# Mixer front of a hybrid encoder trunk: all weight differences on VectorE, long convolution on 24 stretches of 16 tokens

## The chip, the cores and the metric

The kernel runs on one core of one Trainium2 chip. The metric is the device time of one execution in microseconds (us); the time before is the median of three runs. The engines are named as in the profile: PE is TensorE (matmuls), DVE is VectorE, ACT is ScalarE, POOL is GpSimd, SP is SyncE, which issues almost all DMAs.

## The reference

Two layers of a streaming encoder run on 384 tokens: one prompt of 256 tokens and 8 sample streams of 16 tokens. All of it is float32. Cut to what matters:

```
x += 0.5 * rmsnorm(SwiGLU(rmsnorm(x)))          first FFN, D = 1024, D_FF = 2816
n  = rmsnorm(x);  h = n @ w_in                  columns for attention, conv, gMLP, short conv, 4 gates
  a  = latent attention; prompt: softmax over 256 keys in chunks, samples: 256 cached + 16 keys
  xb = ga * sigmoid(gg)                         two 256-channel parts of h
  yb = silu(layernorm(causal_dwconv(concat(buf_b, xb), conv_b_w) + bias))    31 taps per channel
  yc = u * spatial_mix(layernorm(v));  yd = bg * causal_dwconv(cg * hd)      3 taps
  y  = sum_b sigmoid(gate_b) * (branch_b @ w_br_b);  x += rmsnorm(y @ w_o)
x += 0.5 * rmsnorm(SwiGLU(rmsnorm(x)))          second FFN
```

The long convolution (31 taps) reads 30 tokens of history: zeros before the prompt, `state_conv_b` before each sample stream. Its last 30 inputs per stream are outputs too.

## The kernel before

The 384 tokens are three tiles of 128. PE multiplies in a split form: every float32 operand is a rounded high part and the low rest, and three products are added (high x high, low x high, high x low), so each weight is turned into two tiles. A weight unit (mostly 128 x 1024) is loaded by SP into a stage buffer `st` (four buffers, `STAGE`), ACT rounds it into `wh`, and a subtraction `wl = st - wh` gives the rest (`split_unit`, L237). Both lie in a ring in SBUF (`RING_M` KB per partition during the mixer), and PE's products wait for them.

The program is written in the order of a planner's time. `tick` (L184) counts PE's work; what waits for another engine is a generator that goes on when the planner thinks that engine is through. `pump` (L268) prepares the next weight unit when its ring place is free and when ACT and the subtracting engine are at most `BACKLOG` = 400 ns behind, or when fewer than `AHEAD` = 3 units are ready. Each engine then works through its own queue strictly in this order. One list, `self.idle`, holds the taps of the long convolution: `tick` puts one into DVE's queue whenever the planner sees DVE free within 100 ns.

The mixer's front (`mixer_front`) is, in the order of PE: token-major projections (`cq`, then `ckv` and `v`), the first half of the convolution's projections (`conv(0)`), eight query heads (`query`, L934), `conv(1)`, prompt keys and values (`kT`, `v`), then six chains of prompt attention (scores, softmax, transposes, product with `v`) and eight of sample attention, with the remaining feature-major projections (`fillers`) between them. After that comes the merge of the four branches.

From the queries on (`self.pool_split`, L946 to L1167) the subtractions `wl` of the front are POOL's, 20 units per layer; elsewhere they are DVE's. POOL also adds the rotated parts of the queries: two small additions per head, `qTp` and `qr`.

A tap of the long convolution (`taps`, L675) is two instructions for each of two channel chunks: 256 prompt tokens from the buffer `bp` (30 zeros of history, then 256 tokens in a row) and 8 x 16 sample tokens from `bs` (each stream with its own 30 tokens of history). There are 31 taps and two chunks, so 62 taps and 124 instructions per layer; each is `y = x * w + y` with x and y in SBUF, apart from the first tap.

In the rows, `yTb` is the convolution's result, `half` a scratch tile (softmax probabilities among others), `rot` and `acc` PSUM tiles. All instructions of the engines carry line L72, since they are issued through one helper.

Of the kernel before, what the change touches and what calls it, by code (L numbers as in the profile page):

```python
# [16 lines left out]
P = 128  # L17
# [9 lines left out]
S = 16  # L27
PAST = 256
# [10 lines left out]
RING_M = 39  # L39
# [5 lines left out]
POOL_SPLIT = True  # L45
# [14 lines left out]
class Engine:  # L60
    """an engine whose work is counted as it is emitted"""
# [36 lines left out]
class Core:  # L98
# [5 lines left out]
    def plan_units(self):  # L104
        """every weight unit in the order of its use: (key, DRAM AP, shape without partitions)"""
        units = []
        a = self.a
        for l in range(self.depth):
            for f in ("ffn1", "ffn2"):
                if f == "ffn2":  # L110
                    self.plan_mixer(units, l)
                for h in range(4):
                    units.append(((f, l, "s", h), a[f + "_gs"][l, :, 2 * h:2 * h + 2, :], [2, 512],
                                  "F" if f == "ffn2" or l == 0 else "M"))
                order = []
                for c in range(2, NC_FF):
                    order.append(("p", c))
                    if c >= LAG:
                        order.append(("d", c - LAG))
                order += [("d", c) for c in range(NC_FF - LAG, NC_FF)]  # L120
                for k, c in order:
                    if k == "p":
                        for h in range(2):
                            units.append(((f, l, "p", c, h), a[f + "_gp"][l, c - 2, h], [KD, P], "F"))
                    else:
                        units.append(((f, l, "d", c), a[f + "_dn"][l, c * P:(c + 1) * P, :], [D], "F"))
        return units

    # The program is emitted in the order of time. `now` is the tensor engine's work emitted so far, free[e] the time
    # at which another engine is through with its own. What waits for another engine is a generator: it yields the  # L130
    # engine it waits for (or a time) and goes on when that is through, so that others' work comes in between.
# [6 lines left out]
    def spawn(self, name, gen, kind=None):  # L138
        """start a generator; it holds what its parent holds, and the tiles of that kind taken since the last such start"""
        parent = self.cur  # L140
        if parent is None or parent[:len(name)] != name:
            self.seq += 1
            name = name + (self.seq,)
            for slot, names in self.holders.items():
                if parent in names or (parent is None and slot in self.fresh.get(kind, ())):
                    names.add(name)
            self.old.add(kind)
        else:
            name = parent
        busy, self.busy = self.busy, True  # L150
        self.step(name, gen)
        self.busy = busy

    def take(self, slot):
        """before a tile goes into a slot: emit all that still uses the one there"""
        while names := [n for n in self.holders.get(slot, ()) if n != self.cur and self.pending(n)]:
            self.need(names[0])
        self.holders[slot] = {self.cur} - {None}
        if self.cur is None:
            if slot[0] in self.old:  # L160
                self.old.discard(slot[0])
                self.fresh[slot[0]] = set()
            self.fresh.setdefault(slot[0], set()).add(slot)

    def drop(self, kind):
        """the running generator is through with its tiles of that kind"""
# [31 lines left out]
    def need(self, name):  # L198
        """emit until all generators of that name are through"""
# [10 lines left out]
    def wait(self, name, gen):  # L210
        """need(name), with gen's work in between"""
# [25 lines left out]
    def split_unit(self, key, shape, ring, st, n, arrival):  # L237
# [3 lines left out]
        e = POOL if self.pool_split else DVE  # L241
# [4 lines left out]
        getattr(nc, e).tensor_tensor(lo, st, h.bitcast(F32), op=ALU.subtract)  # L246
# [11 lines left out]
    def places(self, ring, n):  # L258
        """where the next two tiles of n bytes lie in the ring, and where it goes on"""
# [8 lines left out]
    def pump(self):  # L268
        """the next unit, if its place in the ring is free by now"""
        if self.next_unit < len(self.units):  # L270
# [5 lines left out]
            lag = max(self.free[ACT], self.free[POOL if self.pool_split else DVE]) - self.now  # L276
# [28 lines left out]
    def mm3(self, out, lhs, rhs, first, last):  # L305
        """out += (lh + ll)^T (rh + rl), without ll rl"""
# [5 lines left out]
    def stat(self, tag, n):  # L312
        """n columns of per-row statistics"""
# [34 lines left out]
    def load_gain(self, ap):  # L348
        """a gain of every column, the same in all partitions"""
# [4 lines left out]
    # The tiles' chains across a boundary: the last products of a sublayer run tile by tile, so a tile's norms  # L354
    # run beside the other tiles' products, and so do the first products of the next sublayer.
    def tails(self, tail, post, gain):
        """tail[t]: the last products of tile t, of its two halves; post: its post-norm; then the pre-norm with gain"""
# [31 lines left out]
    def chain(self, t, post, stats, gain, at=None):  # L389
        """the rest of the post-norm, then xT[:, :, tile t] <- the transpose of the normalised residual"""  # L390
# [65 lines left out]
    def ffn_head(self, f, l):  # L456
        """the first two pairs of gate and up chunks, token-major"""
# [32 lines left out]
    def ffn_body(self, f, l, out=None, hook=None):  # L490
        """the other chunks; returns what the boundary needs: the products left, tile by tile, and the post-norm"""
# [112 lines left out]
    def softmax(self, p, s, n):  # L604
        """p[:, i, :] = softmax of s[:, i, :] over the last axis"""
# [12 lines left out]
    def mixer(self, l, m):  # L618
        """returns what the boundary after it needs"""
# [17 lines left out]
    def mixer_front(self, l, m, mf, ma, aT, yT):  # L637
# [15 lines left out]
        # feature-major projections and the three local branches  # L653
# [12 lines left out]
        bp = mf.tile([P, 2, BW + TP], F32, name="bp")  # L666
        bs_ = mf.tile([P, 2, NB, BW + S], F32, name="bs")
        dp = mf.tile([P, 2, DW + TP], F32, name="dp")
        ds_ = mf.tile([P, 2, NB, DW + S], F32, name="ds")
        nc.gpsimd.memset(bp[:, :, 0:BW], 0.0)  # L670
        nc.gpsimd.memset(dp[:, :, 0:DW], 0.0)
        nc.sync.dma_start(out=bs_[:, :, :, 0:BW], in_=a["stateb"][l])
        nc.sync.dma_start(out=ds_[:, :, :, 0:DW], in_=a["stated"][l])

        def taps(y, pad_p, pad_s, w, ks, bias):  # L675
            for k in ks:
                for e, dst, src in ((nc.vector, y[:, :TP], pad_p[:, k:k + TP]), (nc.vector, samp(y), pad_s[:, :, k:k + S])):
                    wk = w[:, k:k + 1]
                    if k:
                        e.scalar_tensor_tensor(dst, src, wk, dst, op0=ALU.mult, op1=ALU.add)  # L680
                    elif bias is not None:
                        e.tensor_scalar(dst, src, wk, bias, op0=ALU.mult, op1=ALU.add)
                    else:
                        e.tensor_scalar(dst, src, wk, None, op0=ALU.mult)

        y = yT["b"]

# [14 lines left out]
        def conv_glu(c, xa, sg):  # L702
            yield PE
            nc.vector.tensor_tensor(bp[:, c, BW:], xa[:, :TP], sg[:, :TP], op=ALU.mult)
            nc.vector.tensor_tensor(bs_[:, c, :, BW:], samp(xa), samp(sg), op=ALU.mult)
            nc.sync.dma_start(out=a["o_cbp"][l, :, c], in_=bp[:, c, TP:])
            nc.sync.dma_start(out=a["o_cbs"][l, :, c], in_=bs_[:, c, :, S:])
            for k in range(CW):
                self.idle.append(lambda k=k: taps(y[:, c, :], bp[:, c, :], bs_[:, c], cw[:, c, :], [k], cbias[:, c:c + 1]))
# [15 lines left out]
        def short_conv(c, t_, xh_):  # L725
# [3 lines left out]
            taps(yT["d"][:, c, :], dp[:, c, :], ds_[:, c], dw[:, c, :], range(3), None)  # L729
# [36 lines left out]
        def conv_norm():  # L766
            """layer norm over the channels (two partition chunks), then silu"""
# [57 lines left out]
        with pool("mixq") as mq:  # L825
# [6 lines left out]
            # token-major projections: cq | kr, then ckv | v  # L832
# [11 lines left out]
            def latent_q(t):  # L844
# [3 lines left out]
                # the latents' norm, the rotated key part  # L848
# [29 lines left out]
            def latent_kv(t, pb):  # L878
                tt = slice(t * P, (t + 1) * P)
                yield PE  # L880
                # normalised kv latents
# [21 lines left out]
            def gmlp_v(t, pb):  # L903
                """gMLP's normalised v"""
# [26 lines left out]
            # queries: per head 64 nope, 32 rope, the 32 rope columns with their halves swapped  # L931
# [14 lines left out]
            self.pool_split = POOL_SPLIT  # L946
# [15 lines left out]
            # prompt keys and values  # L962
# [30 lines left out]
            # prompt attention  # L993
# [37 lines left out]
            # what the sample attention reads first  # L1031
# [30 lines left out]
        # sample attention, in the latent space; the rope part of four batches runs in four row groups  # L1062
# [104 lines left out]
        self.pool_split = False  # L1167
# [3 lines left out]
    def gate(self, l, c, g, th):  # L1171
        """th = tanh(gate / 2)"""
# [14 lines left out]
    def mixer_merge(self, l, q, aT, yT, mh, ml):  # L1187
        """gates are 2 sigmoid = tanh(g / 2) + 1; the factor 2 goes out in the post-norm"""
# [62 lines left out]
    def rms_stats(self, x, tag):  # L1251
        """the sum of x^2 over its columns, and room for what follows"""
# [4 lines left out]
    def run(self):  # L1257
# [6 lines left out]
        self.pool_split = False  # L1264
# [5 lines left out]
        with ExitStack() as es:  # L1270
# [29 lines left out]
            one = const.tile([P, P], F32, name="one")  # L1300
# [45 lines left out]
class Post:  # L1346
    """x += rmsnorm(h) * gain / 2 for acc = h (FFN); x += rmsnorm(h) * gain for acc = 2 h (mixer)"""
# [35 lines left out]
def lay_out(inp, np):  # L1383
    """the kernel's DRAM arrays: the inputs, re-laid"""
# [51 lines left out]
    # the queries' table carries the scale of the scores  # L1436
# [10 lines left out]
def lay_back(o, np):  # L1447
    """the reference's outputs from the kernel's DRAM arrays"""
# [27 lines left out]
```

## Time and profile before

| | before |
|---|---|
| median of 3 runs | 1942.73 us (1938.77 to 1946.91) |
| span of the profiled execution | 1946.8 us; the run nearest to it is 1946.91 us |
| PE busy | 1883.2 us, 97% |
| DVE busy | 986.1 us, 51% |
| ACT busy | 690.0 us, 35% |
| POOL busy | 155.2 us, 8%, nearly all of it in the two mixer fronts |
| granted TensorE clock, mean | 0.981 |

PE is busy almost throughout; the time that it is not lies in two stretches, the mixer fronts of layer 0 (about 280 to 500 us) and layer 1 (about 1240 to 1465 us). A granted clock of 1 is 2.4 GHz, and 0.5 is 1.2 GHz; a value between them is a mean over a stretch with both.

### The profile page before, as it was taken

The page shows a single profiled execution, that of the slowest core. Times are in us where ns is not written, and L with a number is a line of the kernel's source. Part 1 is how long each engine was busy: PE and PEld are TensorE (multiplying, and loading weights), DVE is VectorE, ACT ScalarE, POOL GpSimd, SP SyncE. Part 2 cuts the span into 40 slices and gives each one's busy share as a digit, 9 for nine tenths or more (in the row PEclk, how much of TensorE's full clock was granted, in tenths as well). Part 3 has the DMA queues.
Part 4 walks back from the last instruction along what each step waited for, and adds up shares of the span by engine and source line. Part 5 has one row for each costly group of instructions (what it writes and reads, how often), then busy time and mean ns, then how long its engine had stood idle before and what let it go on. Part 6 is the DMA issues. An engine that isn't in the chain of part 4 may idle for free.

```text
span 1946.8 us, 25315 instructions
## 1 busy us (share of the span) xinstructions
PE 1883.2 (97%) x10066; PEld 1745.3 (90%) x10066; DVE 986.1 (51%) x1560; ACT 690.0 (35%) x1138; POOL 155.2 (8%) x156
## 2 busy tenths in 40 slices
PE   8999999789999999999999999997899999999998
PEld 7999998677999989999989999986789998899997
DVE  5333357984544473333463333579735444633333
ACT  5333343332433353333343333433223334433322
POOL 0000002522100000000000000025220000000000
PEclk9999999888999999999999999998889999999999
DMA  7434444442343354434444434443423344433341
GB/s 255 131 120 129 127 125 112 117 122 86 106 133 124 115 173 128 129 121 130 130 133 128 130 121 129 127 118 84 138 69 114 114 138 144 141 127 123 130 124 50
DMA packets 99000, 243.13 MB, mean 125 GB/s; under 512 B 29249, under 2 KB 40641, under 8 KB 98882
## 3 DMA queue, kind: packets, MB, share of 16 engines
q1 hardware_dynamic: 98738, 241.45, 40.4%
q8 instruction: 79, 1.29, 0.3%
q14 instruction: 39, 0.32, 0.1%
q10 hardware_dynamic: 144, 0.07, 0.0%
HBM read 237.62 MB, written 3.31 MB: 124 GB/s over the span
## 4 chain that ended last, share of the span: by engine, by line
PE 90%; DVE 9%; issue 1%; ACT 1%; POOL 0%; DMA 0%; POOLq 0%; DVEq 0%; ACTq 0%
PE rot L72 57%; PE acc L72 33%; DVE yTb L72 4%; DVE half L72 1%; DVE yTd L72 1%; DVE qTp L72 0%; DVE sx L72 0%; ACT qTs L72 0%; DVE vn L72 0%; DVE qr L72 0%; DVE xl L72 0%; DVE wl L72 0%; ACT junk L72 0%; DVE kT L72 0%; DVE sv L72 0%
## 5 line engine op out<-in xcount | busy, mean ns | idle before, releaser
L72 DVE TENSOR_TENSOR wl<-st,wh 128x1024 fp32r<-128x1024 f32 (+2 forms) x388 | 456.6, 1185 | 470.2 <-ACT wh L72 449.1
L72 PE MATMUL rot<-xh,wh 128*128 128x384 f32 x1984 | 678.4, 342 | 0.1
L72 PE MATMUL rot<-xh,wl 128*128 128x384 f32 x1984 | 675.6, 341 | 0.0
L72 PE MATMUL rot<-xl,wh 128*128 128x384 f32 x1984 | 674.7, 340 | 0.0
L72 ACT CAST wh<-st 128x1024 fp32r<-128x1024 f32 (+3 forms) x428 | 430.3, 1016 | 668.4 <-issue 374.1
L72 PEld LDWEIGHTS rot<-xh,wh 128*128 128x128 f32 x1984 | 375.7, 189 | 7.4 <-issue 2.9
L72 PEld LDWEIGHTS rot<-xh,wl 128*128 128x128 f32 x1984 | 375.4, 189 | 5.0 <-issue 0.7
L72 PEld LDWEIGHTS rot<-xl,wh 128*128 128x128 f32 x1984 | 375.3, 189 | 2.9 <-issue 1.9
L72 PE MATMUL acc<-wh,hl 128*128 128x512 f32 x528 | 205.8, 390 | 0.0
L72 PE MATMUL acc<-wl,hh 128*128 128x512 f32 x528 | 205.7, 390 | 0.0
L72 PE MATMUL acc<-wh,hh 128*128 128x512 f32 x528 | 205.5, 389 | 0.0
L72 POOL TENSOR_TENSOR post<-post,neghalf 128x1 f32<-128x1 f32 x18 | 12.0, 668 | 1420.2 <-DVE post L72 1420.2
L72 DVE TENSOR_TENSOR hf<-sg,rot 128x384 f32<-128x384 f32 x80 | 44.3, 554 | 152.9 <-PE rot L72 152.9
L72 PEld LDWEIGHTS acc<-wl,hh 128*128 128x128 f32 x528 | 99.1, 188 | 20.5
L72 PEld LDWEIGHTS acc<-wh,hl 128*128 128x128 f32 x528 | 99.1, 188 | 17.6
L72 PEld LDWEIGHTS acc<-wh,hh 128*128 128x128 f32 x528 | 99.1, 188 | 17.6
L72 POOL TENSOR_TENSOR wl<-st,wh 128x1024 fp32r<-128x1024 f32 (+2 forms) x40 | 92.1, 2309 | 182.3 <-ACT wh L72 82.1
L72 DVE SCALAR_TENSOR_TENSOR half<-half,acc 128x384 f32<-128x384 f32 x44 | 24.4, 554 | 140.4 <-PE acc L72 140.4
L72 ACT ACTIVATE half<-rot 128x384 f32<-128x384 f32 x58 | 28.5, 492 | 177.0 <-PE rot L72 177.0
L72 DVE SCALAR_TENSOR_TENSOR yTb<-bp,cols,yTb 128x256 f32<-128x256 f32 x120 | 78.6, 655 | 0.3
L72 PE MATMUL acc<-ident,half 128*128 128x128 f32 (+1 forms) x266 | 44.2, 285 | 20.8 <-DVE half L72 20.8
L72 PEld LDWEIGHTS acc<-ident,half 128*128 128x128 f32 (+1 forms) x266 | 32.9, 142 | 31.8 <-DVE half L72 21.4
(214 smaller groups left out, 1835.5 us busy)
## 6 DMA issues: line engine op xcount, KB each, us to landing
st<-ffn_gp SPq DMA_DIRECT2D x160, 512.0 KB, 3.5
st<-ffn_dn SPq DMA_DIRECT2D x88, 512.0 KB, 3.5
st<-in_g SPq DMA_DIRECT2D x64, 512.0 KB, 4.0
st<-in_f SPq DMA_DIRECT2D x24, 512.0 KB, 3.7
st<-ffn_gs SPq DMA_DIRECT2D x16, 512.0 KB, 4.9
st<-w_o SPq DMA_DIRECT2D x16, 512.0 KB, 4.7
st<-w_br SPq DMA_DIRECT2D x16, 384.0 KB, 3.1
st<-in_b SPq DMA_DIRECT2D x8, 512.0 KB, 4.7
```

Of the source, the lines that this page charges most:

```text
L72: r = f(*args, **kw)
```

## The change

All subtractions `wl` go to DVE, and the planner's lag is that of ACT and DVE. The buffer `bp` is gone: the prompt is held as 16 stretches of 16 tokens, each with its own 30 tokens of history, in front of the 8 sample streams in one buffer `bs` of 24 stretches x 46. DVE writes the 24 x 16 new values in one instruction; ACT then copies each stretch's history out of the stretches before it, in two copies. A tap is one instruction over 24 x 16 = 384 values. The ring for the mixer's weights shrinks from 39 to 36 KB per partition to make room, and a constant tile `one` borrows a scratch tile. Comments are taken out, which changes nothing.

```diff
-RING_M = 39
+RING_M = 36
-POOL_SPLIT = True
@@ split_unit
-        e = POOL if self.pool_split else DVE
...
-        getattr(nc, e).tensor_tensor(lo, st, h.bitcast(F32), op=ALU.subtract)
+        nc.vector.tensor_tensor(lo, st, h.bitcast(F32), op=ALU.subtract)
@@ pump
-            lag = max(self.free[ACT], self.free[POOL if self.pool_split else DVE]) - self.now
+            lag = max(self.free[ACT], self.free[DVE]) - self.now
@@ mixer_front
-        bp = mf.tile([P, 2, BW + TP], F32, name="bp")
-        bs_ = mf.tile([P, 2, NB, BW + S], F32, name="bs")
+        bs_ = mf.tile([P, 2, NP + NB, BW + S], F32, name="bs")
...
-        nc.gpsimd.memset(bp[:, :, 0:BW], 0.0)
+        nc.gpsimd.memset(bs_[:, :, 0, 0:BW], 0.0)
+        nc.gpsimd.memset(bs_[:, :, 1, 0:BW - S], 0.0)
-        nc.sync.dma_start(out=bs_[:, :, :, 0:BW], in_=a["stateb"][l])
+        for c in range(2):
+            nc.sync.dma_start(out=bs_[:, c, NP:, 0:BW], in_=a["stateb"][l, :, c])
...
+        by16 = lambda x: x.rearrange("p (b s) -> p b s", s=S)
+        def tap(c, k):
+            dst, src, wk = by16(y[:, c, :]), bs_[:, c, :, k:k + S], cw[:, c, k:k + 1]
+            if k:
+                nc.vector.scalar_tensor_tensor(dst, src, wk, dst, op0=ALU.mult, op1=ALU.add)
+            else:
+                nc.vector.tensor_scalar(dst, src, wk, cbias[:, c:c + 1], op0=ALU.mult, op1=ALU.add)
@@ conv_glu
-            nc.vector.tensor_tensor(bp[:, c, BW:], xa[:, :TP], sg[:, :TP], op=ALU.mult)
-            nc.vector.tensor_tensor(bs_[:, c, :, BW:], samp(xa), samp(sg), op=ALU.mult)
-            nc.sync.dma_start(out=a["o_cbp"][l, :, c], in_=bp[:, c, TP:])
-            nc.sync.dma_start(out=a["o_cbs"][l, :, c], in_=bs_[:, c, :, S:])
+            w = bs_[:, c]
+            nc.vector.tensor_tensor(w[:, :, BW:], by16(xa), by16(sg), op=ALU.mult)
+            self.drop("rot")
+            yield DVE
+            nc.scalar.copy(w[:, 1:NP, BW - S:BW], w[:, 0:NP - 1, BW:])
+            nc.scalar.copy(w[:, 2:NP, 0:BW - S], w[:, 0:NP - 2, 2 * S:])
+            nc.sync.dma_start(out=a["o_cbs"][l, :, c], in_=w[:, NP:, S:])
+            nc.sync.dma_start(out=a["o_cbp"][l, :, c], in_=w[:, NP - 1, S:])
+            yield ACT
             for k in range(CW):
-                self.idle.append(lambda k=k: taps(y[:, c, :], bp[:, c, :], bs_[:, c], cw[:, c, :], [k], cbias[:, c:c + 1]))
+                self.idle.append(lambda k=k: tap(c, k))
@@ mixer_front, before the queries, and after the front
-            self.pool_split = POOL_SPLIT
...
-        self.pool_split = False
```

The planner writes another order from this. On DVE in layer 0, from the last query head (`half` is its rotated part) to the copies of the prompt's keys `kT`, there stood only taps before (`bp` and `bs`), with the sigmoid `sg` of `conv(1)` and its product between them:

```order
L72 TENSOR_TENSOR half<-acc,rope_f 32x384
L72 SCALAR_TENSOR_TENSOR yTb<-bp,cols,yTb 128x256
L72 SCALAR_TENSOR_TENSOR yTb<-bs,cols,yTb 128x128
...
L72 TENSOR_SCALAR sg<-sg 128x384
...
L72 TENSOR_TENSOR bp<-rot,sg 128x256
L72 TENSOR_TENSOR bs<-rot,sg 128x8x16
...
L72 COPY kT<-acc 64x256 x3
```

Now three subtractions and five taps of the new form stand there:

```order
L72 TENSOR_TENSOR half<-acc,rope_f 32x384
L72 TENSOR_TENSOR wl<-st,wh 128x1024
L72 SCALAR_TENSOR_TENSOR yTb<-bs,cols,yTb 128x384 x2
L72 TENSOR_TENSOR wl<-st,wh 128x1024
L72 TENSOR_SCALAR sg<-sg 128x384
L72 SCALAR_TENSOR_TENSOR yTb<-bs,cols,yTb 128x384 x2
L72 TENSOR_TENSOR wl<-st,wh 128x1024
L72 SCALAR_TENSOR_TENSOR yTb<-bs,cols,yTb 128x384
L72 TENSOR_TENSOR bs<-rot,sg 128x24x16
L72 COPY kT<-acc 64x256
```

Ten taps of two instructions each stood between the last head and the first `kT` copy, and taps stood between the heads too; those between the heads have given way to subtractions.

On POOL in the same place, the end of the queue of the queries was this, with the rotated parts `qTp` and `qr`, nine subtractions in a row, and the copies `cT` of the sample attention:

```order
L72 TENSOR_TENSOR wl<-st,wh 128x1024
L72 TENSOR_TENSOR qTp<-qTp,half 32x256
L72 TENSOR_TENSOR qr_2405<-qr_2405,half 32x8x16
L72 TENSOR_TENSOR wl<-st,wh 128x1024 x9
L72 COPY cT<-latTs 128x2x16 x4
L72 TENSOR_TENSOR wl<-st,wh 128x1024 x2
```

Now the small additions of all heads stand in a row, and nothing else before the copies:

```order
L72 TENSOR_TENSOR sv<-sv,neghalf 128x1
L72 TENSOR_TENSOR kv<-kv,neghalf 128x1
L72 TENSOR_TENSOR qTp<-qTp,half 32x256
L72 TENSOR_TENSOR qr_2405<-qr_2405,half 32x8x16
...
L72 COPY cT<-latTs 128x2x16 x8
```

No subtraction is left on POOL. A third place is DVE at the first softmax of the prompt attention (`sx` its maxima and sums, `half` its probabilities). Before:

```order
L72 MEMSET acc 64x4x64
L72 TENSOR_REDUCE sx<-acc 128x4
L72 SCALAR_TENSOR_TENSOR yTb<-bp,cols,yTb 128x256
L72 SCALAR_TENSOR_TENSOR yTb<-bs,cols,yTb 128x128
...
L72 RECIPROCAL sx<-sx 128x4
L72 TENSOR_SCALAR half<-half,sx 128x128 x4
```

And now:

```order
L72 MEMSET acc 64x4x64
L72 TENSOR_REDUCE sx<-acc 128x4
L72 SCALAR_TENSOR_TENSOR yTb<-bs,cols,yTb 128x384 x2
L72 TENSOR_TENSOR wl<-st,wh 128x1024
L72 MEMSET acc 64x4x64
L72 TENSOR_REDUCE sx<-acc 128x4
L72 RECIPROCAL sx<-sx 128x4
L72 TENSOR_SCALAR half<-half,sx 128x128 x4
```

The second chain's maxima now stand ahead of the first chain's scaling. On PE the transposes that read `half` moved back with it: between the first scores and those transposes stood 26 projection matmuls and one other set of scores before, and now 37 and two. PE's total number of matmuls is the same.

## Rows read from the trace of the kernel before

**Rows 1.** The page: the span of the profiled execution

```profile
span 1946.8 us, 25315 instructions
```

**Rows 2.** Windows: stretch and length, busy us by engine (instructions), granted clock, DMA

```profile
280.00:500.00 220.00, 194.73 (x1084) 169.91 (x1083) 156.98 (x366) 76.69 (x180) 68.24 (x62) 0.92 0.39 105
500.00:1240.00 740.00, 740.00 (x3934) 698.51 (x3934) 332.78 (x409) 265.38 (x387) 8.99 (x15) 1.00 0.41 130
1240.00:1465.00 225.00, 200.50 (x1113) 175.14 (x1113) 162.27 (x373) 81.53 (x186) 69.01 (x62) 0.92 0.37 105
```

**Rows 3.** PE's waits from 290 to 500: total us, times, longest

```profile
PE acc L72 <- DVE kT L72: 10.0, 1, 10.0
PE acc L72 <- DVE half L72: 9.1, 6, 2.3
PE acc L72 <- DVE lat_s L72: 3.1, 1, 3.1
PE acc L72 <- DVE aT L72: 2.0, 1, 2.0
PE acc L72 <- POOL wl L72: 1.0, 2, 0.5
```

**Rows 4.** Timeline of PE at its longest wait: start, duration, operation, idle before

```profile
381.66 2.08 PE L72 MATMUL acc<-kT,qTp 96*128 96x128 f32 x8 [10.00 <-DVE kT L72]
```

**Rows 5.** Timeline of DVE in layer 0's front, single rows: start, duration, operation

```profile
340.49 0.41 DVE L72 TENSOR_TENSOR qTp<-acc,rope_f 96x256 f32<-96x256 f32 x1
342.13 0.42 DVE L72 TENSOR_TENSOR qTp<-acc,rope_f 96x256 f32<-96x256 f32 x1
...
348.19 1.06 DVE L72 SCALAR_TENSOR_TENSOR yTb<-bp,cols,yTb 128x256 f32<-128x256 f32 x1
349.17 0.54 DVE L72 SCALAR_TENSOR_TENSOR yTb<-bs,cols,yTb 128x128 f32<-128x128 f32 x1
...
351.41 0.48 DVE L72 SCALAR_TENSOR_TENSOR yTb<-bp,cols,yTb 128x256 f32<-128x256 f32 x1
...
373.46 2.56 DVE L72 SCALAR_TENSOR_TENSOR yTb<-bp,cols,yTb 128x256 f32<-128x256 f32 x1
375.94 0.34 DVE L72 SCALAR_TENSOR_TENSOR yTb<-bs,cols,yTb 128x128 f32<-128x128 f32 x1
...
389.71 2.96 DVE L72 TENSOR_SCALAR half<-half,sx 128x128 f32<-128x128 f32 x4
...
395.57 0.87 DVE L72 TENSOR_SCALAR half<-half,sx 128x128 f32<-128x128 f32 x4
...
419.87 2.57 DVE L72 SCALAR_TENSOR_TENSOR yTd<-dp,cols,yTd 128x256 f32<-128x256 f32 x1
```

**Rows 6.** Timeline of POOL in the same stretch

```profile
366.02 9.72 POOL L72 TENSOR_TENSOR wl<-st,wh 128x1024 fp32r<-128x1024 f32 x4
...
419.75 2.40 POOL L72 TENSOR_TENSOR wl<-st,wh 128x1024 fp32r<-128x1024 f32 x1 [5.31 <-ACT wh L72]
```

**Rows 7.** Groups by form, whole run: count, busy us, mean ns, idle before

```profile
L72 DVE TENSOR_TENSOR wl<-st,wh 128x1024 fp32r<-128x1024 f32 x346 | 422.2, 1223 | 466.5 <-ACT wh L72 445.4 <-issue 19.5 <-PE acc L72 0.7
L72 DVE SCALAR_TENSOR_TENSOR yTb<-bp,cols,yTb 128x256 f32<-128x256 f32 x120 | 78.6, 655 | 0.3
L72 DVE SCALAR_TENSOR_TENSOR yTb<-bs,cols,yTb 128x128 f32<-128x128 f32 x120 | 53.7, 448 | 0.0
L72 POOL TENSOR_TENSOR qTp<-qTp,half 32x256 f32<-32x256 f32 x16 | 13.0, 810 | 11.1 <-DVE half L72 10.5
```

**Rows 8.** Windows of PE's work right after three waits, columns as above

```profile
346.70:351.50 4.80, 4.80 (x19) 4.72 (x20) 3.97 (x9) 0.81 (x3) 1.76 (x4) 0.64 0.89 286
441.15:445.00 3.85, 3.85 (x24) 3.35 (x25) 2.32 (x8) 0.90 (x4) 0.00 (x0) 1.00 0.53 194
470.04:481.00 10.96, 10.96 (x39) 9.87 (x40) 2.41 (x8) 3.22 (x8) 2.37 (x1) 0.53 0.00 0
```

**Rows 9.** Window from the first query to the start of the sample attention

```profile
337.85:419.50 81.65, 63.33 (x371) 57.14 (x369) 74.03 (x160) 29.87 (x72) 39.48 (x30) 0.90 0.37 104
```

More of the change, by code (lines that the diff above doesn't have):

```diff
@@ L27 @@
 S = 16
+NP = TP // S
 PAST = 256
@@ L665, in mixer_front, with taps @@
         BW, DW = CW - 1, 2
-        bp = mf.tile([P, 2, BW + TP], F32, name="bp")
-        bs_ = mf.tile([P, 2, NB, BW + S], F32, name="bs")
+        bs_ = mf.tile([P, 2, NP + NB, BW + S], F32, name="bs")
         dp = mf.tile([P, 2, DW + TP], F32, name="dp")
         ds_ = mf.tile([P, 2, NB, DW + S], F32, name="ds")
-        nc.gpsimd.memset(bp[:, :, 0:BW], 0.0)
+        nc.gpsimd.memset(bs_[:, :, 0, 0:BW], 0.0)
+        nc.gpsimd.memset(bs_[:, :, 1, 0:BW - S], 0.0)
         nc.gpsimd.memset(dp[:, :, 0:DW], 0.0)
-        nc.sync.dma_start(out=bs_[:, :, :, 0:BW], in_=a["stateb"][l])
+        for c in range(2):
+            nc.sync.dma_start(out=bs_[:, c, NP:, 0:BW], in_=a["stateb"][l, :, c])
         nc.sync.dma_start(out=ds_[:, :, :, 0:DW], in_=a["stated"][l])
-        def taps(y, pad_p, pad_s, w, ks, bias):
-            for k in ks:
-                for e, dst, src in ((nc.vector, y[:, :TP], pad_p[:, k:k + TP]), (nc.vector, samp(y), pad_s[:, :, k:k + S])):
+        def taps(y, pad_p, pad_s, w):
+            for k in range(3):
+                for dst, src in ((y[:, :TP], pad_p[:, k:k + TP]), (samp(y), pad_s[:, :, k:k + S])):
                     wk = w[:, k:k + 1]
                     if k:
-                        e.scalar_tensor_tensor(dst, src, wk, dst, op0=ALU.mult, op1=ALU.add)
-                    elif bias is not None:
-                        e.tensor_scalar(dst, src, wk, bias, op0=ALU.mult, op1=ALU.add)
+                        nc.vector.scalar_tensor_tensor(dst, src, wk, dst, op0=ALU.mult, op1=ALU.add)
                     else:
-                        e.tensor_scalar(dst, src, wk, None, op0=ALU.mult)
+                        nc.vector.tensor_scalar(dst, src, wk, None, op0=ALU.mult)
         y = yT["b"]
+        by16 = lambda x: x.rearrange("p (b s) -> p b s", s=S)
+        def tap(c, k):
+            dst, src, wk = by16(y[:, c, :]), bs_[:, c, :, k:k + S], cw[:, c, k:k + 1]
+            if k:
+                nc.vector.scalar_tensor_tensor(dst, src, wk, dst, op0=ALU.mult, op1=ALU.add)
+            else:
+                nc.vector.tensor_scalar(dst, src, wk, cbias[:, c:c + 1], op0=ALU.mult, op1=ALU.add)
         def conv(c):
@@ L728, in short_conv @@
             nc.vector.tensor_tensor(ds_[:, c, :, DW:], samp(xh_), samp(t_), op=ALU.mult)
-            taps(yT["d"][:, c, :], dp[:, c, :], ds_[:, c], dw[:, c, :], range(3), None)
+            taps(yT["d"][:, c, :], dp[:, c, :], ds_[:, c], dw[:, c, :])
             nc.sync.dma_start(out=a["o_cdp"][l, :, c], in_=dp[:, c, TP:])
@@ L1263, in run @@
         self.spans, self.ring_at, self.size = {"M": {}, "F": {}}, {"M": 0, "F": 0}, {"M": RING_M * 1024, "F": RING_F * 1024}
-        self.pool_split = False
         self.now, self.seq, self.busy, self.queue, self.idle = 0.0, 0, False, [], []
@@ L1299, in run @@
             es.enter_context(tc.manual_schedule(engines=ENGINES))
-            one = const.tile([P, P], F32, name="one")
+            one = self.half()[:, :P]
             nc.vector.memset(one[0:1], 1.0)
```

## Prediction

> **What bounds the kernel now.** First the windows by stage [rows 2]: between the two mixer fronts PE is busy for all of 740.0 us at a clock of 1.00, so nothing that leaves PE's work alone can shorten that part. In the fronts PE is idle for 220.0 - 194.7 = 25.3 us and 225.0 - 200.5 = 24.5 us, and the clock is 0.92. The change touches the fronts alone, so 49.8 us of idle time and what the clock costs there are all that it can win.
>
> Second, PE's waits in layer 0 [rows 3]: 10.0 us for the prompt's keys `kT`, 9.1 us in six waits for `half`, 3.1 for `lat_s`, 2.0 for `aT`, 1.0 for POOL's `wl`. Nearly all are waits for DVE, which from the first query to the sample attention is busy for 74.0 of 81.7 us [rows 9].
>
> Third, why DVE is late. A tap lasts 0.48 us on 256 tokens and 0.34 on 128 when it is alone; from 366.0 to 375.7, where POOL does four subtractions in 9.72 us, taps last about 2.5 us, as long as one of POOL's subtractions [rows 5, 6]. The two longest single waits of DVE's other customers have the same face: four scalings of `half` take 2.96 us at 389.71 and 0.87 at 395.57, and at 419.87 a short-convolution tap takes 2.57 us while POOL subtracts from 419.75 on [rows 5, 6]. What gets stretched reads SBUF on both sides or is a scaling within SBUF; instructions that read PSUM, as `qTp`, keep their 0.41 [rows 5]. By the means, the 60 taps on `bp` per layer lose 60 x (0.655 - 0.475) = 10.8 us and those on `bs` 60 x (0.448 - 0.342) = 6.4 [rows 5, 7].
>
> Fourth, the clock. After the 3.1 us wait PE works at 0.64 for 4.8 us, after the last wait for `half` at 0.53 for 11.0 us, and after one of 1.9 us at 1.00 [rows 8]. Five such stretches in layer 0, from the first to the last of these, lose 4.80 x 0.36 = 1.7 to 10.96 x 0.47 = 5.2 us each, 13.8 together. The mean clock of layer 1's front is the same 0.92 [rows 2], so I take 13.8 there too: 27.6.
>
> **The change part by part.**
>
> *Subtractions to DVE.* Twenty per layer, 17 of 1024 columns at 1.22 us [rows 7], which follow each other every 1.15 (each instruction overlaps the next by some 0.08, as the rows' starts show), and three smaller at about 0.8: 22 us more for DVE per layer. Out go the stretched instructions: 17.2 us on the taps, and some 8 us of single rows like 389.71 and 419.87 [rows 5]: 25 us.
>
> *One tap instead of two.* From one start to the next a pair takes 0.40 + 0.26; 128 columns cost 0.34 against 0.48 for 256, so 0.14 per 128, and one of 384 columns takes 0.53. That saves 0.13 x 62 = 8 us per layer. No row shows 24 stretches of 16; the nearest is `bs` itself, 8 stretches of 16 with gaps, whose 0.34 lies on the line of the contiguous taps less 128 columns. Bounds: 0.40 (as 256 columns) and 0.66 (as the pair); I take 0.53. DVE's balance per layer is 22 - 25 - 8 = -11 us, so it gets freer while doing more.
>
> *ACT's copies.* Four per layer, of 240 and 196 columns, which no row shows; even at DVE's 0.53 us for 384 columns they are 2.1 us, and ACT is busy for only 76.7 of the front's 220.0 us [rows 2]; that they gain something is excluded, since nothing like them went out of ACT's queue. The first taps wait for them, and one subtraction, already due, stands between on DVE. On SP the outputs of the state wait behind these copies too, with four stage buffers ahead: 0, at worst 1 us per layer. The split state load moves the same bytes. The ring of 36 KB holds nine tiles of 4 KB, as that of 39 did; the smaller merge units are taken a little later, where PE has never waited [rows 2]: 0, at worst 2 us.
>
> *The keys.* PE comes to the first scores at 381.66 - 10.0 = 371.7 [rows 4]; without the waits for `lat_s` and `wl` and the slow stretch (3.1 + 1.0 + 1.7) at 365.9. DVE starts the query heads at 340.5 and takes 342.13 - 340.49 = 1.64 us for each, 13.1 for eight [rows 5]. Up to the first `kT` copy its new queue holds six subtractions (5 x 1.15 + 0.9 = 6.7), five taps (2.7), the norms of `vn` and `lat_s` (0.8), `sg` and `bs` (0.8): 24.1, so 364.6, and 1.3 for two copies and the tap between: 365.9. The tie leaves no margin: the small additions on POOL stay, and stretched a pair of taps by 1.06 + 0.54 - 0.48 - 0.34 = 0.8 us at 348.19 [rows 5]. Four subtractions now stand between heads and can be held so: 0 to 3.1 us. PE's own residual wait for `lat_s` of about 1.2 takes part of that. I take a wait of 1.5 for `kT`.
>
> The Trainium skill ("SBUF — State Buffer", section "Who interferes with whom") says that a DVE instruction with two SBUF inputs and a GpSimd instruction that reads SBUF exclude each other for the whole instruction, whoever came first. The trace agrees (taps of 2.5 us beside 2.4 us of POOL). The rule speaks against part of this change: a moved subtraction has two SBUF inputs and the additions remain, so each of the four could be held for a whole pair of them, 0.81 + 0.50; by it the wait for `kT` would be up to 3.6 and the sum 4 us less.
>
> *What is late next.* DVE's queue is nearly as full as PE's from the first query on: 74.0 us of work less some 11, against PE's 63.3 [rows 9], so DVE sets the pace at times. The new weight units come through the same queue: 0.8 us of waits per layer instead of 1.0. The softmax chains get more room (37 matmuls and two scores instead of 26 and one before the first transposes), but share DVE with 12 subtractions: 3 us per layer instead of 11.1. After the last tap DVE had been half idle.
>
> *Sum.* Waits left per layer: 1.2 + 1.5 + 0.8 + 3 = 6.5; saved 18.8 + 18.0 = 36.8. Clock: with most waits under 2 us, one middling slow stretch (3 us) is left per layer; saved 27.6 - 6 = 21.6. Together 58.4: the profiled execution of 1946.8 [rows 1] becomes 1888.4. It lies 4.1 above the median, so the forecast is 1942.7 - 58.4 = **1884 us**. Its own range is 1868 (13 us of waits and 6 of clock fall to almost nothing) to 1899.
>
> **Rivals.**
>
> *DVE becomes the bound.* The front's queue has no slack (above), and the planner takes a query head for less than the 1.64 us that it needs. If the backlog lasts to the end of the prompt attention, half the waits and half the slow stretches stay: 24.9 + 13.8 = 38.7 won, 1904. Against it: taps are the filler, and become fewer.
>
> *Weights late behind taps.* If each of 20 units makes PE wait for a subtraction and a tap (1.15 + 0.53 = 1.7 us), 34 us of waits per layer come, too short for the clock to fall: 1942.7 - 77.4 + 68 = 1933. For it: POOL had these units almost to itself. Against: at least three units are kept ready.
>
> *Slower: the 24 stretches.* If a tap pays at each start of a stretch, all 62 stand in a queue that PE waits for. The gain of 29 us per layer is gone at 29 / 62 = 0.47 us more per tap, a tap of 1.0 us; with 1.5 us it is 60 us lost per layer: 1942.7 - 58 + 120 = 2005. The 8 stretches of `bs` speak against it.
>
> *It does not free DVE.* If the remaining additions or something else stretch the taps as much, only POOL's 1.0 us per layer go: 1941. The 9.72 us of POOL beside four stretched taps speak against it.
>
> **How the numbers follow.** Forecast 0.75, DVE-bound 0.15, late weights 0.04, nothing freed 0.03, slower 0.03. A change under 0.5% (9.7 us) can't be told from none. Faster takes the first two, 0.90; within 0.5% gets 0.06 with the next two, slower 0.04. The range ends at 1865 below (all 49.8 + 27.6 = 77.4 gone) and above at 1914, beyond the DVE-bound case and short of late weights.
>
> **What would show it.** POOL's busy time falls from 155 us by 40 subtractions of about 2.3, to some 63. No tap lasts over 1.3 us, and one on 384 columns has a mean near 0.61. PE's wait for `kT` is under 4 us and its idle time in each front under 10; the clock in both fronts is above 0.97. A tap near 1 us, PE waits on `wl` by DVE of over 10 us in all, or a `kT` wait still near 10 would prove the steps wrong.

## The result and the profile after

The changed kernel takes 1888.33 us (1885.2 to 1890.9, four runs) beside 1942.85 for the kernel before on the same chip: a ratio of 0.971, with an interval from 0.969 to 0.974. Two later sets of runs, on other occasions, gave it 1886.5 (ratio 0.970, 0.967 to 0.973) and 1886.6 (0.971, 0.969 to 0.973). The forecast was 1884, with a range of 1865 to 1914.

The page first: its span, and each engine's busy time, share and instructions.

```profile
span 1883.4 us, 25172 instructions
...
PE 1858.1 (99%) x10066; PEld 1723.3 (91%) x10066; DVE 964.1 (51%) x1472; ACT 693.3 (37%) x1146; POOL 73.8 (4%) x118
```

The profiled span fell by 63.4 us [rows 1], the medians by 54.5. A span is some 2 us shorter than the time of the same execution (1883.4 beside 1885.2 here), so the profiled run of before stood about 6 us above its median, and this one 3 below its own. The windows by stage answer to [rows 2]; columns as there. The fronts have become shorter, so their windows are too.

```profile
280.00:490.00 210.00, 203.78 (x1209) 180.65 (x1208) 160.80 (x340) 86.40 (x196) 28.60 (x43) 1.00 0.43 123
490.00:1210.00 720.00, 720.00 (x3817) 677.88 (x3816) 319.11 (x393) 258.87 (x376) 7.69 (x14) 1.00 0.41 130
1210.00:1430.00 220.00, 214.20 (x1268) 190.86 (x1267) 166.76 (x348) 89.70 (x201) 28.53 (x43) 1.00 0.40 116
```

PE is idle for 6.2 and 5.8 us in the two fronts instead of 25.3 and 24.5, and the granted clock is 1.00 (2.4 GHz) in both instead of 0.92. Of the 63.4 us, 49.8 - 12.0 = 37.8 are idle time that went from the fronts. Nearly all of the other 25.6 is PE's busy time, 1883.2 before and 1858.1 now for the same number of matmuls: the matmuls of the fronts ran at a higher granted clock.

PE's waits of layer 0's front, in the view of [rows 3]:

```profile
PE acc L72 <- DVE half L72: 3.2, 5, 1.6
PE acc L72 <- DVE qa L72: 0.9, 1, 0.9
PE rot L72 <- ACT sg L72: 0.7, 1, 0.7
```

The wait of 10.0 us for `kT` is gone, and so is that for `wl`. No wait is longer than 1.6 us here, or 1.7 in layer 1. The groups by form, as in [rows 7]:

```profile
L72 DVE TENSOR_TENSOR wl<-st,wh 128x1024 fp32r<-128x1024 f32 x380 | 463.7, 1223 | 477.1 <-ACT wh L72 475.3 <-issue 0.7
L72 DVE SCALAR_TENSOR_TENSOR yTb<-bs,cols,yTb 128x384 f32<-128x384 f32 x120 | 74.8, 623 | 2.2
L72 POOL TENSOR_TENSOR qTp<-qTp,half 32x256 f32<-32x256 f32 x16 | 19.1, 1191 | 11.8 <-DVE half L72 11.8
L72 POOL COPY cT<-latTs 128x32 f32<-128x32 f32 x16 | 6.8, 445 | 128.7 <-PE acc L72 128.6
```

The 34 subtractions that moved left the mean of DVE's at 1223 ns, and none in either front lasts over 1227: none is held. A tap on 384 columns lasts 0.62 us. But POOL's addition to `qTp`, 810 ns before, now lasts 1191. The timeline shows why (start, duration, idle before); first POOL, then DVE:

```profile
348.10 0.73 POOL L72 TENSOR_TENSOR qTp<-qTp,half 32x256 f32<-32x256 f32 x1 [0.51 <-DVE half L72]
...
349.77 1.78 POOL L72 TENSOR_TENSOR qTp<-qTp,half 32x256 f32<-32x256 f32 x1 [0.52 <-DVE half L72]
...
358.97 1.77 POOL L72 TENSOR_TENSOR qTp<-qTp,half 32x256 f32<-32x256 f32 x1 [0.51 <-DVE half L72]
```

```profile
349.72 1.23 DVE L72 TENSOR_TENSOR wl<-st,wh 128x1024 fp32r<-128x1024 f32 x1
...
360.06 1.83 DVE L72 SCALAR_TENSOR_TENSOR yTb<-bs,cols,yTb 128x384 f32<-128x384 f32 x2
...
363.25 1.26 DVE L72 SCALAR_TENSOR_TENSOR yTb<-bs,cols,yTb 128x384 f32<-128x384 f32 x2
...
366.79 0.42 DVE L72 COPY kT<-acc 64x256 f32<-64x256 f32 x1
...
378.09 0.87 DVE L72 TENSOR_SCALAR half<-half,sx 128x128 f32<-128x128 f32 x4
```

The addition that starts 0.05 us after DVE's subtraction takes 1.05 us longer than the free one; the subtraction keeps its 1.23. The contention is still there, mostly with the other engine as the loser, and nobody waits for POOL at this place. DVE loses once in each layer: an addition that was itself held ends at 360.74, and the first of the two taps at 360.06 takes 1.09 us, the longest tap of the run, so that the pair takes 1.83 instead of 1.26. The four scalings that took 2.96 us before [rows 5] take 0.87.

### The profile page after: what moved, and what is told of

Read it like the earlier page. It is cut to its first block, busy times and chain, and to the rows that moved or that the text cites. A ratio compares the mean times of both kernels' runs of the same rounds, so it can differ in the third digit from the quotient of the medians.

```text
span 1883.4 us, 25172 instructions
## 1 busy us (share of the span) xinstructions
PE 1858.1 (99%) x10066; PEld 1723.3 (91%) x10066; DVE 964.1 (51%) x1472; ACT 693.3 (37%) x1146; POOL 73.8 (4%) x118
## 4 chain that ended last, share of the span: by engine, by line
PE 92%; DVE 6%; ACT 1%; issue 1%; POOL 0%; DMA 0%; POOLq 0%; DVEq 0%; ACTq 0%
PE rot L72 59%; PE acc L72 33%; DVE yTb L72 1%; DVE wl L72 1%; DVE half L72 1%; DVE sx L72 0%; ACT half L72 0%; DVE sv L72 0%; DVE qTp L72 0%; DVE xl L72 0%; DVE yTd L72 0%; DVE qa L72 0%; DVE kT L72 0%; POOL kv L72 0%; ACT qTs L72 0%
## 5 line engine op out<-in xcount | busy, mean ns | idle before, releaser
L72 DVE TENSOR_TENSOR wl<-st,wh 128x1024 fp32r<-128x1024 f32 (+3 forms) x428 | 502.2, 1184 | 481.8 <-ACT wh L72 479.0
L72 PEld LDWEIGHTS acc<-wh,hl 128*128 128x128 f32 x528 | 99.1, 188 | 17.6
L72 DVE SCALAR_TENSOR_TENSOR yTb<-bs,cols,yTb 128x384 f32<-128x384 f32 x120 | 74.8, 623 | 2.2
L72 PE MATMUL rot<-wl,xh 128*128 128x512 f32 (+1 forms) x144 | 55.8, 388 | 1.5 <-DVE wl L72 1.5
L72 PE MATMUL rot<-wh,xh 128*128 128x512 f32 (+1 forms) x144 | 56.2, 390 | 0.0
```

The costliest lines, as they stand in the source:

```text
L72: r = f(*args, **kw)
```

## The experiments

The theory: POOL's subtractions, which read SBUF, stretched DVE's SBUF-to-SBUF instructions; DVE was late; PE waited for it, and after the waits ran at a low clock. The rivals: one tap in place of two is what freed DVE; or the order of the instructions, or late weights from POOL, cost the time. The table gives each kernel's median, its ratio to the runs of before beside it with the interval, PE's idle time in both fronts, and the rest of the profiled span (the same 10066 matmuls in all, so the rest grows when the clock is lower). The last two columns are of one profiled execution each.

| kernel | us | ratio | idle, fronts | span less idle |
|---|---|---|---|---|
| before | 1942.9 | 1 | 49.8 | 1897.0 |
| changed | 1888.3 | 0.971 (0.969 to 0.974) | 12.0 | 1871.4 |
| only subtractions moved | 1891.2 | 0.972 (0.970 to 0.975) | 14.5 | 1874.7 |
| only taps changed | 1939.6 | 0.998 (0.997 to 0.999) | 42.3 | 1894.3 |
| changed, POOL reads added | 1924.7 | 0.989 (0.986 to 0.992) | 34.6 | 1883.8 |
| changed, POOL fills added | 1902.8 | 0.978 (0.976 to 0.980) | 22.7 | 1878.6 |
| changed, adds to DVE | 1895.9 | 0.975 (0.972 to 0.978) | 17.6 | 1874.7 |
| the same, planned so | 1895.5 | 0.975 (0.972 to 0.977) | 16.0 | 1878.0 |
| changed, contiguous taps | 1891.0 | 0.972 (0.969 to 0.975) | 11.4 | 1877.8 |
| changed, ACT's copy last | 1883.8 | 0.969 (0.967 to 0.971) | 9.9 | 1873.7 |

### Only the subtractions moved

The kernel before, with

```
-POOL_SPLIT = True
+POOL_SPLIT = False
```

> The kernel before with one change: all weight subtractions of the fronts on VectorE. The long convolution keeps its pair of taps (prompt, samples), the ring its 39 KB. Theory (the POOL subtractions stretched DVE's SBUF-to-SBUF instructions, and DVE made PE wait): nearly all of the 54 us is won by this part alone; DVE has 62 x (0.66 - 0.53) = 8 us more per layer than in the changed kernel, so 1895, between 1888 and 1905; taps on 256 and 128 columns near 0.48 and 0.34 us, clock in the fronts at 0.98 or more. Rival (one tap instead of two is what freed DVE): little won, 1925 to 1943.

Measured: 1891.2 us, as the theory had it: this part alone wins 51 of the 54 us. The planner also writes another order here, so this run by itself doesn't part contention from order. The taps, as pairs again, last what those that met no POOL instruction lasted in the kernel before, 0.48 and 0.34 us [rows 5] (by form):

```profile
L72 DVE SCALAR_TENSOR_TENSOR yTb<-bp,cols,yTb 128x256 f32<-128x256 f32 x120 | 58.4, 487 | 0.0
L72 DVE SCALAR_TENSOR_TENSOR yTb<-bs,cols,yTb 128x128 f32<-128x128 f32 x120 | 41.6, 347 | 0.0
```

655 ns became 487 and 448 became 347 [rows 7] with no edit to the taps.

### Only the taps changed

The changed kernel, with POOL's subtractions of the fronts back:

```
+        e = POOL if self.pool_split else DVE
...
-        nc.vector.tensor_tensor(lo, st, h.bitcast(F32), op=ALU.subtract)
+        getattr(nc, e).tensor_tensor(lo, st, h.bitcast(F32), op=ALU.subtract)
```

> The changed kernel with its subtractions of the fronts put back on POOL; the one tap on 24 stretches and the ring of 36 KB stay. Theory: the contention is back, so the taps on 384 columns that meet a POOL subtraction last about 2.4 us and the waits for kT and half return; there are half as many taps to stretch, so 1930, between 1915 and 1943. Rival (the taps are what won): 1888 to 1900.

Measured: 1939.6 us, a gain of 0.2%, at the upper end of what the theory gave. The single tap is stretched as the pair was, and the long waits are there again (by form, and PE's waits from 290 to 500):

```profile
L72 DVE SCALAR_TENSOR_TENSOR yTb<-bs,cols,yTb 128x384 f32<-128x384 f32 x120 | 99.8, 831 | 2.9
```

```profile
PE acc L72 <- DVE half L72: 6.7, 5, 3.2
PE acc L72 <- DVE kT L72: 5.6, 1, 5.6
PE acc L72 <- DVE lat_s L72: 4.2, 1, 4.2
```

With the run above, the rival of the taps falls: the one tap won almost nothing as long as POOL subtracted, and 3 to 5 us after that (1891.2 against 1886.5 to 1888.3, with intervals of the ratios that overlap).

### POOL reads, and nobody needs the result

These two runs ask whether contention alone makes the loss, with PE's, DVE's and ACT's instructions in the order of the changed kernel. Behind each moved subtraction of the fronts stands one more line:

```
+        if self.pool_split:
+            self.tc.nc.gpsimd.tensor_tensor(st, st, st, op=ALU.subtract)
```

> The changed kernel, and after each weight subtraction of the fronts an added one on POOL, of the stage buffer with itself in place (128x1024, two SBUF inputs), whose result nobody reads. No engine waits for it but the next load into that buffer; PE's instructions stand in the order of the changed kernel. Theory (a POOL instruction that reads SBUF holds DVE's): taps of 2 us and more, PE's waits and the low clock come back although no product needs POOL: 1945, between 1925 and 1980. Rival (what cost time before was that PE's weights came late from a slow POOL, or the order of the instructions): no change, 1885 to 1893.

Measured: 1924.7 us; the added work costs 36 to 38 us. That is a little under the expected range and far from the rival's 1893. Taps of 2 us came back (the longest is 2.13), the low clock only in part: it is 0.98 in each front, against 0.92 before. One stretch of POOL, and DVE in the same microseconds:

```profile
362.15 2.09 POOL L247 TENSOR_TENSOR st<-st 128x1024 f32<-128x1024 f32 x1
364.32 1.59 POOL L72 TENSOR_TENSOR qTp<-qTp,half 32x256 f32<-32x256 f32 x1
...
366.52 2.09 POOL L247 TENSOR_TENSOR st<-st 128x1024 f32<-128x1024 f32 x1
```

```profile
362.41 2.91 DVE L72 TENSOR_TENSOR wl<-st,wh 128x1024 fp32r<-128x1024 f32 x1
...
366.05 2.98 DVE L72 SCALAR_TENSOR_TENSOR yTb<-bs,cols,yTb 128x384 f32<-128x384 f32 x2
```

DVE's subtraction starts 0.26 us after POOL's and takes 2.91 us instead of 1.23; two taps take 2.98 instead of 1.26. So a moved subtraction can be held after all, when POOL is first. PE's `half` waits are 7.4 us in each front, against 3.2 and 1.7.

### POOL fills, and reads nothing

```
-            self.tc.nc.gpsimd.tensor_tensor(st, st, st, op=ALU.subtract)
+            self.tc.nc.gpsimd.memset(st, 0.0)
+            self.tc.nc.gpsimd.memset(st, 0.0)
```

> As the run with the added POOL subtraction, but in its place POOL fills the same stage buffer with zeros twice (128x1024 each, about 2 us together by the 0.535 us of a fill of 512 columns): as long busy on POOL, but reading nothing. Theory (reading is what holds DVE): taps near 0.62 us, 1885 to 1895. Rival (any POOL instruction on SBUF holds DVE): as the other run, 1925 or more.

Measured: 1902.8 us, between the two expectations, and both missed something. On the taps the theory is right: their mean is 632 ns, and six in a row keep their pace while POOL fills from 409.86 to 411.8. The scalings of the softmax are another matter. POOL, then DVE:

```profile
396.09 0.95 POOL L247 MEMSET st<- 128x1024 f32 x1 [4.66 <-DVE wl L72]
397.10 0.98 POOL L248 MEMSET st<- 128x1024 f32 x1
...
409.86 0.95 POOL L247 MEMSET st<- 128x1024 f32 x1 [7.75 <-DVE wl L72]
410.86 0.95 POOL L248 MEMSET st<- 128x1024 f32 x1
```

```profile
392.67 0.62 DVE L72 TENSOR_SCALAR half<-half,sx 128x256 f32<-128x256 f32 x2
...
396.36 1.87 DVE L72 TENSOR_SCALAR half<-half,sx 128x256 f32<-128x256 f32 x2
...
409.72 3.88 DVE L72 SCALAR_TENSOR_TENSOR yTb<-bs,cols,yTb 128x384 f32<-128x384 f32 x6
```

Two scalings take 1.87 us beside the fills and 0.62 without, and a scaling has one input in SBUF and its output there. The Trainium skill ("SBUF — State Buffer", section "Who interferes with whom") says that a DVE instruction with two SBUF inputs contends with a GpSimd instruction that reads SBUF, not with one that only writes it, and that `tensor_scalar` can enter a mode that uses both of VectorE's port pairs, the one shared with GpSimd too, and then contends with it. The rows of this run agree with both: the taps kept their pace beside the fills and the scalings did not. In which mode the scalings ran no row shows.

Another part of the loss comes through POOL's own queue. The fills put its additions off, and some now come ahead of a DVE instruction that they followed in the changed kernel. POOL, then DVE:

```profile
354.50 0.73 POOL L72 TENSOR_TENSOR qTp<-qTp,half 32x256 f32<-32x256 f32 x1
```

```profile
354.51 1.81 DVE L72 TENSOR_TENSOR wl<-st,wh 128x1024 fp32r<-128x1024 f32 x1
```

This subtraction takes 1.81 us instead of 1.23. And the copies of `cT` stand behind fills, and PE waits for them, 2.8 us in each layer.

```profile
PE acc L72 <- DVE half L72: 3.9, 5, 2.1
PE acc L72 <- POOL cT L72: 2.8, 1, 2.8
```

That wait is 3.0 us with the reads, so this part costs the same in both runs. SP, too, waits about as long in both until POOL is through with a stage buffer (75.6 us with the reads and 78.5 with the fills, from 300 to 480), so late loads aren't what parts them. What reading costs beyond filling, for nearly the same time on POOL (149.5 and 142.4 us busy), is then 1924.7 - 1902.8 = 22 us.

### The last two POOL instructions to DVE

The rope additions of the queries are what still contends. They were put on VectorE, once with the planner left as it is (the order of PE and ACT is kept), once counted by it:

```
-                nc.gpsimd.tensor_tensor(qTp[64:96, h, :], qTp[64:96, h, :], rt[64:96, :TP], op=ALU.add)
-                nc.gpsimd.tensor_tensor(qr, qr, bsv(rt[64:96, TP:T]), op=ALU.add)
+                tc.nc.vector.tensor_tensor(qTp[64:96, h, :], qTp[64:96, h, :], rt[64:96, :TP], op=ALU.add)
+                tc.nc.vector.tensor_tensor(qr, qr, bsv(rt[64:96, TP:T]), op=ALU.add)
```

> The changed kernel with the queries' two small additions (32x256 and 32x8x16) on VectorE instead of POOL; PE's and ACT's instructions stand in the same order. Theory of contention: the taps of 1.1 us go, but so do POOL's cover and 16 additions of some 0.3 to 0.4 us come into DVE's full queue, 5 us per layer ahead of kT, of which PE waits for 1 to 3: 1886 to 1893, most likely 1889. Rival (DVE's queue has room, and what is left of the front's 12 us of idle is due to the additions being held on POOL): 1880 to 1885.

> The same two additions on VectorE, and counted there by the planner, which then also puts PE's, ACT's and VectorE's instructions into another order. If the planner's cost is what was off, a better order: 1882 to 1887. If not, as with the order held, 1886 to 1893.

Measured: 1895.9 and 1895.5 us, 9 us slower than the changed kernel beside them, and more than either expectation. The intervals of the ratios overlap a little (0.972 to 0.978 and 0.967 to 0.973), but the fastest of the eight runs, 1894.1, is slower than the slowest of the changed kernel's, 1892.1. No tap is now over 0.62 us; DVE's queue is simply longer (first run):

```profile
363.34 1.22 DVE L72 TENSOR_TENSOR wl<-st,wh 128x1024 fp32r<-128x1024 f32 x1
364.60 0.42 DVE L955 TENSOR_TENSOR qTp<-qTp,half 32x256 f32<-32x256 f32 x1
364.94 0.28 DVE L956 TENSOR_TENSOR qr<-qr,half 32x128 f32<-32x128 f32 x1
...
371.40 0.43 DVE L72 COPY kT<-acc 64x256 f32<-64x256 f32 x1
```

The first copy of a key comes at 371.4 instead of 366.8, PE waits 1.0 us for `kT` and, new, 2.9 for `wl` in layer 0. The planned order does no better. So DVE's queue ahead of the keys has no room for 5 us of additions, and a held POOL is the better place for them.

### Contiguous taps, and the changed kernel again

```
-            dst, src, wk = by16(y[:, c, :]), bs_[:, c, :, k:k + S], cw[:, c, k:k + 1]
+            flat = bs_[:, c].rearrange("p b s -> p (b s)")
+            dst, src, wk = y[:, c, :], flat[:, k:k + T], cw[:, c, k:k + 1]
```

> The changed kernel with the taps of the long convolution on 384 contiguous columns of the padded buffer instead of 24 stretches of 16, which leaves the history out of the convolution. If 24 starts cost something, a tap falls from 0.62 to the 0.58 or less that 256 columns (0.48) and 0.1 for 128 more give; if not, it stays at 0.61 to 0.63. Either way the time stays near 1888 (1884 to 1891), since taps fill DVE's gaps.

> The changed kernel itself once more, as the measure for the small differences of the three other runs beside it: 1888, between 1885 and 1891. Against the run that has the subtractions on VectorE and the pair of taps (1891.2) it says what the one tap is worth: if DVE's time there is hidden, 0 to 4 us.

Measured: 1891.0 and 1886.5 us. Tap by tap there is no difference: 74.8 us for 120 and a mean of 623 ns in both kernels, so 24 stretches of 16 with gaps cost nothing over 384 contiguous columns. (The 0.58 of the expectation was too low a mark: the line through 256 and 128 columns gives 0.62.) The waits are the same too, but the clock in layer 1's front was granted at 0.97 in this execution:

```profile
1210.00:1430.00 220.00, 214.74 (x1236) 190.33 (x1235) 162.91 (x343) 86.58 (x197) 28.50 (x43) 0.97 0.40 116
```

### ScalarE's copy of a query head last

In every query head of the changed kernel, as before it, DVE stands still for 0.34 us behind its first product, until ACT has made `qTs` from the same PSUM tile. One line was moved behind DVE's three products; every engine's order stays as it was.

```
-                nc.scalar.mul(qTs[i * 64:(i + 1) * 64, hp, :], o[0:64, TP:], SM_SCALE)
...
                 nc.vector.tensor_tensor(rt[64:96, :T], o[96:128, :], self.rope_f[96:128, :], op=ALU.mult)
+                nc.scalar.mul(qTs[i * 64:(i + 1) * 64, hp, :], o[0:64, TP:], SM_SCALE)
```

> The changed kernel with one line of each query head moved: ScalarE's scaled copy qTs of the head is emitted behind VectorE's three products instead of between them, so that VectorE no longer waits 0.34 us in each head for ScalarE to be through with the same bank (16 waits in all in the trace of the changed kernel); every engine's instructions stand in the same order. Theory (VectorE's queue from the first query to the first softmax sets what PE still waits for): 2.7 us less in each layer ahead of the keys, of which PE can gain 0 to 2 us per layer: 1883 to 1888, against 1887 to 1888 for the changed kernel. Rival (PE is the bound there, the keys being in time by now): no change, 1886 to 1890.

> The changed kernel itself, beside the run with the moved copy: 1887, between 1885 and 1890.

Measured: 1883.8 us against 1886.6 beside it, the ratios 0.969 (0.967 to 0.971) and 0.971 (0.969 to 0.973). It is the lowest median of all the kernels, and lower by the 3 us that the theory allowed. The intervals of the ratios overlap, though none of its five runs (1882.4 to 1885.4) is as slow as the fastest of the four beside them (1885.6 to 1891.1): a gain of some 3 us is likely, but these few runs don't settle it. What it does inside is plain in DVE's timeline: a head without the gap, and the first key copy 2.5 us earlier.

```profile
346.55 0.56 DVE L72 TENSOR_TENSOR half<-acc,rope_f 32x384 f32<-32x384 f32 x1
347.14 0.42 DVE L72 TENSOR_TENSOR qTp<-acc,rope_f 96x256 f32<-96x256 f32 x1
347.57 0.29 DVE L72 TENSOR_TENSOR qr<-acc,rope_f 32x128 f32<-32x128 f32 x1
347.89 0.56 DVE L72 TENSOR_TENSOR half<-acc,rope_f 32x384 f32<-32x384 f32 x1
...
364.27 0.43 DVE L72 COPY kT<-acc 64x256 f32<-64x256 f32 x1
```

PE's idle time in layer 0 falls from 6.2 to 4.4 us by it: the `half` wait is 1.7 us instead of 3.2.

## Why the prediction was right, point by point

*The cause.* Right, and shown from both sides: without POOL's subtractions and with the old taps the time goes, and with POOL's reads put back beside DVE's subtractions, in the same order of PE, DVE and ACT, two thirds of it come back (36 us). Of these, 22 are what reading adds to filling; the other 14 come with the fills as well; the rows name held scalings, additions that come first and the copies of `cT` as ways, without a price for each. What isn't separated is the third that is left (1924.7 against 1942.9): there POOL's subtractions also delayed weights, and the order was another.

*Idle time.* 6.5 us left per layer were forecast, 6.2 and 5.8 were measured; 36.8 us saved, against 37.8. The parts of that sum are less good than the sum, so that it fits is in part luck. The 1.5 us for `kT` did not come, nor the 0.8 for weights, and `lat_s` cost 0.3 and 0.5 instead of 1.2. The softmax chains cost 3.2 and 1.7 where 3 was taken. What made up for it is a row of waits of 0.4 to 1.7 us (`qa`, `sg`, `pTs`, `sx`, in layer 1 `latTs`) that the sum did not name.

*The keys.* The forecast had a tie at 365.9, and it was a tie, 1.5 us later. DVE's first copy began at 366.8 (forecast 364.6), and PE had no gap ahead of its scores, which began at 367.4. No pair of additions held a subtraction ahead of the keys; one addition held a tap, for half a microsecond. The Trainium skill's rule ("SBUF — State Buffer", "Who interferes with whom"), that whoever comes first keeps the other out for its whole instruction, was weighed against the change in one direction only. Here the additions follow DVE's products at once, and a subtraction that stands next in DVE's queue starts before them (349.72 against 349.77). The rows of both directions exist in these runs, the 1.78 us of POOL here and the 2.91 of DVE in the run with POOL's reads.

*The clock.* The term that was mis-sized, twice. One slow stretch of 3 us was left in each layer by the forecast, and in the profiled execution there was none: 25.6 us beside the idle time were won between the two profiled runs, instead of 21.6. But the loss of 27.6 was read from one execution of before, with a mean clock of 0.981. Its span, 1946.8, was set against the median of times, 1942.7, as 4.1 above it, where it is about 6; in other executions of that kernel, those near 1941 us, the clock is 0.986 to 0.988, so there was less to win than the profile showed. The forecast took the profile's 58.4 us from the median all the same, and the medians fell by 54.5. The idle time of the other executions isn't known; if it is that of the profiled ones, the clock gave 54.5 - 37.8 = 16.7 us between the medians. That is 4.9 less than the 21.6 of the forecast, against 1.0 more of idle time, which makes the 4 us between forecast and result.

*DVE's balance.* The 11 us per layer came out as (986.1 - 964.1) / 2 = 11.0, but by two errors. The subtractions alone brought (986.1 - 974.7) / 2 = 5.7, where 25 - 22 = 3 was taken: with the 22 for the subtractions that came, some 28 per layer went out with the contention. And the single tap brought (974.7 - 964.1) / 2 = 5.3 instead of 8. Its 0.53 us from start to start holds only when something else follows it (335.14 to 335.67 us, for one, in the changed kernel). In a row each tap reads what the last has written, and six take 3.88 us, so (3.88 - 0.62) / 5 = 0.65 each, the price of the pair. In the pair, prompt and samples took turns, and the overlap was there.

*POOL.* Busy for 73.8 us instead of 63. The 10.8 us are its `qTp` additions (16 x 0.38 = 6.1), the `cT` copies (6.8 - 3.5 = 3.3), the other addition of each head, `qr` (0.7), and that to `kv` (0.5): the held side of the same contention, which the forecast kept at the old durations.

*No tap over 1.3 us, a mean near 0.61.* The longest is 1.09, the mean 0.62. *The costs taken as nothing*: ACT's copies last 0.40 and 0.36 us, and no wait of PE names them or the ring.

*The rivals.* DVE as the bound was the nearest: the run with the additions on DVE reached it with 5 us more in that queue, and cost 9. The 24 stretches cost nothing, and in the changed kernel no weights came late behind taps; with the additions on DVE PE waited 2.9 us for weights.

## What to carry to other kernels

Before giving GpSimd elementwise work to relieve VectorE, look in the timeline at what VectorE does in the same microseconds. If its instructions there have two SBUF inputs and the GpSimd work reads SBUF, VectorE can lose more time by being held than it saves: here taking back 22 us of subtractions per layer made its busy time shorter, by 5.7 us. Where both must run at once, let the engine that nobody waits for be the one that starts second, as POOL's additions did here. Two short instructions merged into one save their fixed cost only where the merged ones don't depend on each other in a row.

## What the runs showed that was not expected

POOL's fills hold DVE's one-input scalings (1.87 us against 0.62 for two) and leave the taps alone, so "POOL touches SBUF" is too coarse and "POOL reads SBUF" too narrow.

A chain of dependent taps runs at 0.65 us from start to start, a tap followed by other work at 0.53, although both show the same 0.62 in the groups: the mean duration hides it.

The clock in a front was not the same in each execution with the same waits: 1.00 and 0.97 in layer 1 of two kernels whose longest wait there was 1.7 us. The loss in the second lies from 1380 to 1400, where the clock is 0.66 and PE is busy for all of the 20 us; in the 20 us before, it had waited 0.4 in both kernels. So a low clock does not always follow a long wait, and a clock term read from the waits alone, as in the prediction, can miss. Which of the two a run gets is not settled here; for one front of 220 us it is worth some 6 us (1877.8 against 1871.4 for the span less idle time).
